# The last expert but one spread by a one-hot product, and the end of the kernel put in another order

## The chip, the cores and the metric

The kernel runs on one core of a Trainium2 chip. Its time is the device time of one execution in microseconds (us); the median of three runs stands for it. Engines are named as in the profile: PE is TensorE (matmuls), DVE is VectorE, ACT is ScalarE, POOL is GpSimd, SP is SyncE, which issues most DMAs. Each engine works through its own instructions in order; what waits at its head holds up all that stands behind.

## The reference

One layer of a latent backbone for 512 tokens of 1024 features: a gated linear attention mixer, then a mixture of 16 experts of which each token uses two, and a last RMSNorm. The change is in the experts and in the norm:

```python
for e in range(N_EXPERTS):
    he = jax.nn.silu(h @ w1[e]) * (h @ w3[e])
    out = out + gates[:, e:e + 1] * (he @ w2[e])
...
x = x + g2 * f.reshape(bsz, t, D_MODEL)
return _rmsnorm(x, final_g)
```

Each expert's w1, w3 and w2 are 2 MB each in float32, so all experts together read 96 MB.

## The kernel before

The experts are worked through one after another, the fullest ones first; which expert stands at which of the last 14 places is found at run time. In this text "expert 13" is the one at place 13 of the list `ex`, so experts 14 and 15 are the last two, with room for 32 tokens each; expert 13 has room for 64. Weights come in units of 1 MB, two for each of the parts a, b (gate and up weights, first and second half of the 1024 inputs) and d (down weights). `load_unit` issues a unit from SP; a manual dependency makes it wait until the unit three places back (two, from the 88th on) has landed. Units 88 and 89 are expert 14's d, 90 and 91 expert 15's a, 92 and 93 its b, 94 its first half of d; the other half comes as two half units.

Experts with more than 64 tokens (`Tile_`) have their weights split into a high and a low part on ACT and DVE (lines 56 and 57) and take three matmuls for one. Small experts (`Part`) use raw float32 weights (line 1202). Their tokens are gathered from `h2d` by POOL, turned on PE (1194), multiplied (1202), copied by ACT (`act`, 1210), turned again (1215), passed through SiLU on ACT and a product on DVE (`tr`, 1218 and 1219), multiplied with d, and scaled by the gate on DVE (`store`, 1227 or 1233). POOL then adds the rows into `accd` in DRAM by an indirect DMA (`scatter`, 1106). One scatter waits for the one before it.

At the end, `finish_load` reads the four tiles of 128 tokens back from `accd` (SP, line 1342), after the last scatter has landed; ACT sums their squares (`squares`, 1345); DVE scales them and SP writes them out. Expert 15 is not scattered: its rows of `accd` are gathered (`late_rows`), its own result is added (1381), these rows are normed by themselves and written over the output's rows by an indirect DMA (`late_store`, 1393). `finish_consts` sets aside freed weight buffers for all this and lays two constant rows out for expert 15 (`lay`, ACT copies of 32x256).

A list of small DVE steps, "bookkeeping" below, prepares a loop for tokens beyond the experts' room (lines 1457 to 1490); it stands behind `ex[10]`. With these inputs the loop runs zero times. Inside `manual_schedule(engines=tail)` the order of the code is the order on the engines; elsewhere a scheduler sets it.

Of the kernel before, what the change touches and what calls it, by code (L numbers as in the profile page):

```python
# [8 lines left out]
F32 = mybir.dt.float32  # L9
# [23 lines left out]
def dit_kernel(ctx: ExitStack, tc: tile.TileContext, I, out):  # L33
# [647 lines left out]
    def load_unit(u, e, s, hs=None):  # L681
        t = u[s] if s in u else free.pop(0)
        if t is None:
            t = stg.tile([P, 2048], F32, tag="st", name="st")
        w, v = (I[("w_gate_e", "w_up_e")[s % 2]], s // 2) if s < 4 else (I["w_down_e"], s - 4)
        w = w[0, e, v] if isinstance(e, int) else w[0, bass.ds(e, 1), v].rearrange("a p n -> (a p) n")
        h = slice(0, 2048) if hs is None else slice(1024 * hs.start, 1024 * hs.stop)
        d = nc.sync.dma_start(t[:, h], w[:, h])
        if len(dmas) >= 3 and not isinstance(e, int):
            back = 2 if hs is not None or len(dmas) >= 88 else 3  # L690
            tc.add_manual_dep(d.ins, dmas[-back].ins.name, mybir.DependencyInfo(mybir.DependencyClass.Sync, mybir.DependencyReason.DATA), reason="queue depth")
        dmas.append(d)
        u[s] = t
# [488 lines left out]

    class Part:
        def __init__(s, c, w):
            s.idx, s.gs, s.late, s.mark = gix2[:, c:c + 1], gsl[:, c:c + 1], None, None
# [26 lines left out]
        def tr(s):  # L1212
            pt = bank(pb)
            for k in range(s.nk):
                PE.transpose(pt[:, k * P:(k + 1) * P], s.he[:, k * P:(k + 1) * P], ident)
            pt = pt[:, 0:s.n].rearrange("p (k a t) -> p k a t", k=s.nk, a=s.A)
            s.hr = s.he[:, 0:s.n // 2].rearrange("p (k a t) -> p k a t", k=s.nk, a=s.A // 2)
            S.activation(s.hr, pt[:, :, 0:s.A // 2], AF.Silu)
            V.tensor_mul(s.hr, s.hr, pt[:, :, s.A // 2:s.A])
            s.py = bank()[:, 0:s.n]  # L1220

        def dn(s, kt, w):
# [90 lines left out]
    one = raw2[0:1, :]  # L1313
    ss3, rstd3 = R("ss3", [4]), R("rstd3", [4])
    fin = {}

    def finish_consts():
        f, e = free.pop(0), free.pop(0)
        fin["g"], fin["j"], fin["row"] = f[:, 0:1024], f[:, 1024:2048], f[0:1, 1024:2048]
        fin["y"], fin["z"] = [[u[:, h * 1024:h * 1024 + 1024] for u in (free.pop(0), free.pop(0)) for h in range(2)] for _ in range(2)]  # L1320
        fin["h"], fin["g2"], fin["y15"] = [e[:, k * 512:k * 512 + 512] for k in range(3)]
# [10 lines left out]
    def finish_g():  # L1332
        for a in range(2):
            sl = slice(a * 512, a * 512 + 512)
            pt = bank()
            PE.matmul(pt, one, fin["row"][:, sl], start=True, stop=True)
            S.copy(fin["g"][:, sl], pt)
        lay("h", fin["g"])
# [8 lines left out]
    def finish_rsqrt(t):  # L1347
        rsqrt(rstd3[:, t:t + 2], ss3[:, t:t + 2], 2, 1.0 / D, "a", between=(lambda: finish_mul(3)) if t else None)

    def finish_mul(t):  # L1350
        (V if t % 2 else G).tensor_mul(fin["z"][t], fin["y"][t], fin["g"])

    def finish(t):
        z, r = fin["z"][t], rstd3[:, t:t + 1]
        V.tensor_scalar(z, z, r, None, op0=OP.mult)
        nc.sync.dma_start(out[0, t * P:(t + 1) * P, :], z)

    def finish_half(t):
        squares(t)
        finish_mul(t)  # L1360
        if t == 0:
            finish_mul(1)
        squares(t + 1)
        finish_rsqrt(t)
        finish(t)
        finish(t + 1)

    QA = P // tiles[-1][2]
    SELP = wr.rearrange("p k e -> p (k e)")
# [3 lines left out]
        V.tensor_add(sv, sv, ia) if a else V.tensor_copy(sv, ia)  # L1373
    lrs = R("lrs", [1])

    def late_rows(t):
        t.z = xbuf()[:, 0:t.n]
        gather(t.z, parts(accd, t.A), t.idx, t.A * T)

    def late_add(t):  # L1380
        V.tensor_add(t.z, t.z, t.y)
# [39 lines left out]
    with tc.manual_schedule(engines=tail):  # L1421
        p_, q_ = ex[NE - 2:]
        p, q = p_.tls[0], q_.tls[0]
        p.late = mo.tile([P, D], F32, tag="t4", name="y", bufs=NY)[:, 0:p.n]
        q.late = fin["y15"][:, 0:q.n]
# [6 lines left out]
        for c in "uFab":  # L1432
            if c == "F":
                finish_load()
            elif c in "0123":
                finish_load([int(c)])
            else:
                load_unit(wts[NE - 1], regs[NE - 1], {"u": 4}.get(c, 5), {"a": range(1), "b": range(1, 2)}.get(c))
        late_rows(q)
# [12 lines left out]
    ctx2.enter_context(tc.issue_after(ex[10].mark.ins))  # L1452
    NB = 9
    cap = R("cap", [NE])
    tmp4 = rk16
# [20 lines left out]
    t64 = big2[:, 0:64]  # L1476
    for x in range(NB):
        V.scalar_tensor_tensor(t64, cr, float(x + 1), capb.rearrange("p b e -> p (b e)"), op0=OP.is_equal, op1=OP.mult)
        V.tensor_reduce(off[:, x:x + 1], t64, axis=AX.X, op=OP.add)
        V.tensor_scalar(t64, cr, float(x + 1), None, op0=OP.is_equal)  # L1480
        V.tensor_reduce(ohe[:, x], t64.rearrange("p (b e) -> p e b", b=4), axis=AX.X, op=OP.add)
        ob = ohe[:, x].unsqueeze(1).to_broadcast([P, 4, NE])
        V.tensor_mul(tmp4.rearrange("p (t e) f -> p t (e f)", t=4), zm, ob)
        V.tensor_reduce(pmo[:, x], tmp4.rearrange("p (t e) f -> p t (e f)", t=4), axis=AX.X, op=OP.add)
        V.tensor_mul(tmp4.rearrange("p (t e) f -> p t (e f)", t=4), oh[:, 1], ob)
        V.tensor_reduce(k1o[:, x], tmp4.rearrange("p (t e) f -> p t (e f)", t=4), axis=AX.X, op=OP.add)
# [53 lines left out]
```

## Time and profile before

| | us |
|---|---|
| median of three runs | 655.16 (655.14 to 655.5) |
| the profiled execution's own time | 656.5 |
| its span, first to last instruction | 654.7 |
| PE busy | 599.0 (91%) |
| DVE busy | 463.6 (71%) |
| ACT busy | 302.6 (46%) |

The profile shows one execution. A busy PE is one with matmuls in flight, which is not the same as PE at its peak; the granted clock stands in a column of its own. Busy shares are means over stages with different limits, so the end is read by itself below.

### The profile page before, as it was taken

To read this page: it belongs to the slowest core of one execution; us is meant where nothing else is said; L and a number is where in the kernel's file an instruction comes from. 1 tells how busy PE (TensorE), PEld (TensorE's weight loads), DVE (VectorE), ACT (ScalarE), POOL (GpSimd) and SP (SyncE) were. 2 spreads that over 40 slices of the span, in tenths; PEclk is the share of its full clock that TensorE was granted. 3 is DMA by queue.
4 is the path that set the end of the run, shared out by engine and by line. 5 is a ranking of instruction groups with operands and counts; after the bars stand their busy time and mean duration, and the time that the engine had idled before them with its cause. 6 is when DMAs were issued, how large, how long until landed. Compare 5 with 4: busy or idle time off the path is not lost. (4 is left out here: it accounts for less than half of the span.)

```text
span 654.7 us, 11203 instructions
## 1 busy us (share of the span) xinstructions
PE 599.0 (91%) x4200; PEld 412.4 (63%) x4200; DVE 463.6 (71%) x984; ACT 302.6 (46%) x511; POOL 98.3 (15%) x102
## 2 busy tenths in 40 slices
PE   3999999999999999999979989999999999999741
PEld 2778577776878878778748465545565657664310
DVE  5667499849985972575288399465767689999615
ACT  6433399257352233642451255334444457773131
POOL 4030000010100010012200330120322222222032
PEclk9999999999999999999998999999999999999975
DMA  8996472220234861658662989899999999999974
GB/s 269 340 353 218 175 274 66 67 66 4 67 130 158 270 232 51 254 183 354 237 227 74 373 316 366 326 342 351 412 387 395 362 352 358 393 383 345 298 273 189
DMA packets 50251, 168.41 MB, mean 257 GB/s; under 512 B 6779, under 2 KB 17237, under 8 KB 37138
## 3 DMA queue, kind: packets, MB, share of 16 engines
q1 hardware_dynamic: 43216, 156.26, 64.4%
q0 software_dynamic: 5024, 8.70, 5.6%
q10 hardware_dynamic: 1954, 2.71, 1.3%
q8 instruction: 34, 0.56, 0.3%
q14 instruction: 23, 0.19, 0.1%
HBM read 158.64 MB, written 12.30 MB: 261 GB/s over the span
## 5 line engine op out<-in xcount | busy, mean ns | idle before, releaser
L51 PE MATMUL bk<-wh,fh 128*128 128x512 f32 (+3 forms) x276 | 110.9, 409 | 0.7 <-ACT fh L56 0.4
L52 PE MATMUL bk<-wl,fh 128*128 128x512 f32 (+3 forms) x276 | 111.3, 405 | 0.0
L53 PE MATMUL bk<-wh,fl 128*128 128x512 f32 (+3 forms) x276 | 109.0, 399 | 0.5 <-DVE fl L57 0.5
L282 DVE TENSOR_TENSOR wl<-st,wh 128x512 fp32r<-128x512 f32 x60 | 39.9, 685 | 38.9 <-ACT wh L281 37.6
L56 ACT CAST wh<-su 128x1024 fp32r<-128x1024 f32 x45 | 46.8, 1047 | 39.9 <-PE bk L53 38.7
L281 ACT CAST wh<-st 128x512 fp32r<-128x512 f32 x60 | 35.9, 620 | 59.5 <-PE bk L53 50.8
L51 PEld LDWEIGHTS bk<-wh,fh 128*128 128x128 f32 (+3 forms) x276 | 50.2, 183 | 19.2 <-ACT wh L56 3.3
L57 DVE TENSOR_TENSOR wl<-su,wh 128x1024 fp32r<-128x1024 f32 x45 | 54.5, 1222 | 10.5 <-ACT wh L56 8.3
L1106 POOL DMA_INDIRECT accd<-y,gix x16 | 37.2, 2324 | 164.8 <-DVE y L1166 78.2
L52 PEld LDWEIGHTS bk<-wl,fh 128*128 128x128 f32 (+3 forms) x276 | 50.6, 183 | 16.5 <-issue 3.3
L53 PEld LDWEIGHTS bk<-wh,fl 128*128 128x128 f32 (+3 forms) x276 | 50.6, 183 | 13.7 <-issue 1.2
L1202 PE MATMUL bk<-su,he 128*64 128x512 f32 (+1 forms) x136 | 21.7, 526 | 12.5 <-DMA su<-in_w_down_e_dram 9.6
L1202 PE MATMUL bk<-su,xg 128*32 128x256 f32 (+1 forms) x216 | 31.7, 485 | 1.5 <-DVE xg L1196 1.5
L56 ACT CAST fx<-su 128x1024 fp32r<-128x1024 f32 x21 | 22.0, 1050 | 21.8 <-PE bk L53 21.6
L57 DVE TENSOR_TENSOR fx<-su,fx 128x1024 fp32r<-128x1024 f32 x21 | 25.7, 1222 | 7.4 <-ACT fx L56 7.2
L51 PE MATMUL bk<-fx,fh 128*128 128x512 f32 (+3 forms) x68 | 27.9, 410 | 1.2 <-ACT fh L56 1.2
L52 PE MATMUL bk<-fx,fh 128*128 128x512 f32 (+3 forms) x68 | 27.3, 402 | 1.0 <-DVE fx L57 1.0
L53 PE MATMUL bk<-fx,fl 128*128 128x512 f32 (+3 forms) x68 | 26.6, 394 | 0.2 <-DVE fl L57 0.2
L1102 POOL DMA_INDIRECT xg<-h2d,gix x16 | 20.1, 1259 | 39.2 <-DVE pis L1005 15.1
L250 POOL DMA_DIRECT2D mrd<-mrow x8 | 3.8, 487 | 129.2 <-DVE mrow L248 129.2
L1202 PEld LDWEIGHTS bk<-su,he 128*64 128x64 f32 (+1 forms) x136 | 6.6, 127 | 24.4 <-DMA su<-in_w_down_e_dram 11.0
L57 DVE TENSOR_TENSOR fl<-bk,fh 128x512 fp32r<-128x512 f32 (+3 forms) x25 | 15.5, 634 | 7.5 <-ACT fh L56 5.5
(476 smaller groups left out, 1303.6 us busy)
## 6 DMA issues: line engine op xcount, KB each, us to landing
su<-in_w_up_e_dram SPq DMA_DIRECT2D x23, 1024.0 KB, 8.2
su<-in_w_down_e_dram SPq DMA_DIRECT2D x21, 1024.0 KB, 7.8
su<-in_w_gate_e_dram SPq DMA_DIRECT2D x19, 1024.0 KB, 8.3
st<-in_gla_w_in_dram SPq DMA_DIRECT2D x10, 1024.0 KB, 5.0
QQ<-in_w_mod_dram SPq DMA_DIRECT2D x5, 1024.0 KB, 10.8
st<-in_w_gate_e_dram SPq DMA_DIRECT2D x5, 1024.0 KB, 6.8
st<-in_w_up_e_dram SPq DMA_DIRECT2D x5, 1024.0 KB, 9.0
B<-in_w_mod_dram SPq DMA_DIRECT2D x4, 1024.0 KB, 5.1
```

Of the source, the lines that this page charges most:

```text
L51: PE.matmul(o, ah, bh, start=first, stop=False)
L52: PE.matmul(o, ah, bl, start=False, stop=False)
L53: return PE.matmul(o, al, bh, start=False, stop=last)
L56: S.copy(hi, full)
L57: return V.tensor_sub(lo, full, hi.bitcast(F32))
L250: G.dma_start(mrd[4 * h_ + c4:4 * h_ + c4 + 1, :], mrow[32 * c4:32 * c4 + 1, :])
L281: S.copy(w[0][:, k], st[:, k])
L282: mark[0] = V.tensor_sub(w[1][:, k], st[:, k], w[0][:, k].bitcast(F32))
L1102: G.indirect_dma_start(out=xg, out_offset=None, in_=src, in_offset=bass.IndirectOffsetOnAxis(ap=idx, axis=0), bounds_check=n - 1, oob_is_e ...
L1106: G.indirect_dma_start(out=dst, out_offset=bass.IndirectOffsetOnAxis(ap=idx, axis=0), in_=y, in_offset=None, bounds_check=n - 1, oob_is_er ...
L1202: PE.matmul(o[s.w * a:s.w * a + s.w], l, r(a), start=first, stop=last, tile_position=(0, s.w * a))
```

## The change

- Queue depth: a unit's load waits for the unit three places back to the very end.
- Expert 14 is no longer scattered. Its result `p.late` is put as a high and a low half into two zeroed tiles of 128x1024 (`spread_pads`); a one-hot matrix of its token numbers spreads the rows over each of the four tiles of tokens by float32r matmuls (`spread_mm`, eight for the first two tiles between expert 15's parts a and b, eight behind them), and DVE adds them from PSUM to the tiles read back (`spread_add`). `finish_load` then waits for expert 13's scatter as the last one.
- Expert 15's rows are picked out of the four finished sums on PE by a second one-hot matrix (`late_rows`), not gathered from DRAM.
- The final norm's weights come by a DMA of 512 KB that repeats the row on all partitions (issued by ACT), in place of a row of 4 KB and matmuls with ones; they are laid out for expert 15 at the same place in `finish_consts`.
- Expert 15's SiLU is made from an exponential, an addition, a reciprocal and a product (`by_exp`); ACT's table is changed ahead of it. The final scaling is one DVE step for each tile instead of two; POOL no longer multiplies.
- The bookkeeping takes three blocks at a time and stands behind `ex[4]`.

```diff
-            back = 2 if hs is not None or len(dmas) >= 88 else 3
+            back = 3
...
+            if s.by_exp:
+                S.activation(s.hr, gate, AF.Exp, scale=-1.0)
+                V.tensor_scalar(s.hr, s.hr, 1.0, None, op0=OP.add)
+                V.reciprocal(s.hr, s.hr)
+                V.tensor_mul(s.hr, s.hr, gate)
...
     def finish_consts():
...
-        nc.scalar.dma_start(fin["row"], I["final_g"].rearrange("(o n) -> o n", o=1))
-        V.memset(one, 1.0)
+        nc.scalar.dma_start(fin["g"], I["final_g"].rearrange("(o n) -> o n", o=1).partition_broadcast(P))
         lay("g2", g2b)
+        lay("h", fin["g"])
...
+    def finish_out(t):
+        z = fin["y"][t]
+        V.scalar_tensor_tensor(z, z, rstd3[:, t:t + 1], fin["g"], op0=OP.mult, op1=OP.mult)
         nc.sync.dma_start(out[0, t * P:(t + 1) * P, :], z)
...
+    def spread_pads(t):
+        ph, pl = spread[0]
+        for a in range(t.A):
+            q, n = slice(t.w * a, t.w * a + t.w), slice(a * t.n, a * t.n + t.n)
+            S.copy(ph[q, n], t.y[q])
+            V.tensor_sub(pl[q, n], t.y[q], ph[q, n].bitcast(F32))
+
+    def spread_mm(k):
+        (ph, pl), hot = spread
+        bs = [bank(), bank()]
+        for a, b in enumerate(bs):
+            for p_, f in ((ph, True), (pl, False)):
+                PE.matmul(b, hot[:, k * P:k * P + P], p_[:, a * 512:a * 512 + 512], start=f, stop=not f)
+        return bs
+
+    def spread_add(k, bs):
+        for a, b in enumerate(bs):
+            y = fin["y"][k][:, a * 512:a * 512 + 512]
+            V.tensor_add(y, y, b)
...
-    def late_rows(t):
-        t.z = xbuf()[:, 0:t.n]
-        gather(t.z, parts(accd, t.A), t.idx, t.A * T)
+    def late_rows(t, k):
+        if k == 0:
+            t.rows = bank(pb)[:, 0:t.n]
+        t.groups(t.rows, fin["hot"][:, k], lambda a: fin["y"][k][:, a * t.n:a * t.n + t.n], k == 0, k == 3)
...
         p_.down(wts[NE - 2])
-        p_.scatter()
-        G.drain()
-        finish_g()
+        S.preload_act_table_set("natural_log_exp_and_others")
         q_.up(wts[NE - 1], "a")
+        spread_pads(p)
+        load_unit(wts[NE - 1], regs[NE - 1], 4)
+        finish_load()
+        for h in range(2):
+            load_unit(wts[NE - 1], regs[NE - 1], 5, range(h, h + 1))
+        bs = [spread_mm(k) for k in range(2)]
         q_.up(wts[NE - 1], "b")
...
         q_.turn()
-        S.preload_act_table_set("natural_log_exp_and_others")
-        for h in range(2):
-            finish_half(2 * h)
+        for k in range(2):
+            spread_add(k, bs[k])
+            squares(k)
+        bs += [spread_mm(k) for k in range(2, 4)]
+        for k in range(2):
+            late_rows(q, k)
+        finish_scale(0)
+        for k in range(2, 4):
+            spread_add(k, bs[k])
+            squares(k)
+            late_rows(q, k)
+        finish_out(0)
+        finish_out(1)
+        finish_scale(2)
         q_.down(wts[NE - 1])
         late_add(q)
         late_square(q)
+        finish_out(2)
+        finish_out(3)
         late_out(q)
         late_store(q)
...
-    ctx2.enter_context(tc.issue_after(ex[10].mark.ins))
+    ctx2.enter_context(tc.issue_after(ex[4].mark.ins))
```

**ACT around expert 13's turn.** Before, these rows stand on ACT one after another: `lay` of the gate row (1330), the DMA of the 4 KB row (1322), expert 13's `act` (1210) and its SiLU (1218). The names in brackets are the counters that a row waits for; DMAHW stands for a DMA of SP or ACT.

```order
L1330 COPY srg<-g1b 32x256 [waits DMAHW6_49,PE_49]
L1330 COPY srg<-g1b 32x256 x3
L1322 DMA srg<-in_final_g_dram 1x1024 [waits DMAHW5_49,DMAHW2_49,PE_49]
L1210 COPY he<-bk 128x512 [waits PE_49]
L1218 ACTIVATE he<-bk 128x256 [waits PE_49,Activation_49]
```

In the change the same place on ACT reads as follows (line 1330 is now the DMA of the final norm's weights, 1338 is `lay`, 1225 is expert 13's SiLU).

```order
L1330 DMA srg<-in_final_g_dram 128x1024 [waits DMAHW5_49,DMAHW1_49,PE_49]
L1338 COPY srg<-g1b 32x256 [waits DMAHW6_49,PE_49]
L1210 COPY he<-bk 128x512 [waits PE_49]
L1338 COPY srg<-g1b 32x256 x3
L1338 COPY srg<-srg 32x256 [waits DMAHW1_49]
L1338 COPY srg<-srg 32x256 x3
L1225 ACTIVATE he<-bk 128x256 [waits PE_49,Activation_49]
```

Four copies that read the landed weights (srg from srg, waiting for a DMA) now stand ahead of expert 13's SiLU.

**DVE from expert 15's turn on.** In the change DVE's rows at the end are these (1221 to 1226 are expert 15's SiLU and product, 1392 the additions of the spread rows, 136 to 129 the steps of the reciprocal root).

```order
L1221 TENSOR_SCALAR he<-he 128x128 [waits Activation_49]
L1222 RECIPROCAL he<-he 128x128 [waits DVE_49]
L1223 TENSOR_TENSOR he<-he,bk 128x128 [waits DVE_49,PE_49]
L1226 TENSOR_TENSOR he<-he,bk 128x128 [waits DVE_49]
L1392 TENSOR_TENSOR B_86<-B_86,bk 128x512 [waits DMAHW7_49,DMAHW5_49]
L1392 TENSOR_TENSOR B_86<-B_86,bk 128x512
L1392 TENSOR_TENSOR B_86<-B_86,bk 128x512 [waits DMAHW6_49]
L1392 TENSOR_TENSOR B_86<-B_86,bk 128x512
L136 TENSOR_SCALAR rsv<-ss_3376 128x2 [waits Activation_49]
L127 TENSOR_TENSOR rst<-rstd_3377 128x2 [waits Activation_49]
```

Before, expert 15's one product (1219) stood there, and right behind it the first product of the final scaling; all additions of the spread rows now stand behind expert 15's turn.

## Rows read from the trace of the kernel before

**Rows 1.** Stages by engine: window, length, busy times, PE's clock, DMA share, GB/s.

```profile
572.00:588.00 16.00, 15.70 (x72) 9.98 (x71) 15.71 (x23) 12.61 (x14) 3.50 (x3) 1.00 1.00 385
601.40:608.00 6.60, 6.06 (x53) 2.37 (x53) 6.46 (x41) 2.19 (x5) 1.46 (x1) 1.00 0.94 296
624.00:630.00 6.00, 4.24 (x46) 1.69 (x38) 0.00 (x0) 0.37 (x1) 1.56 (x1) 0.85 0.68 222
636.00:642.00 6.00, 1.08 (x8) 0.20 (x8) 5.58 (x7) 4.34 (x10) 4.11 (x2) 0.50 0.83 301
```

**Rows 2.** The end in time order: start, length, instruction, idle time before it and releaser.

```profile
630.26 2.03 SPq L1342 DMA_DIRECT2D B<-accd  x2
634.11 1.06 ACT L1345 ACTIVATE srg<-B 128x1024 f32<-128x1024 f32 x1 [2.43 <-issue]
642.51 1.08 PE L1202 MATMUL bk<-su,he 128*32 128x256 f32 x8 [0.74 <-DMA su<-in_w_down_e_dram]
645.74 0.48 DVE L1227 SCALAR_TENSOR_TENSOR srg<-bk,gsl,srg 128x256 f32<-128x256 f32 x1
647.89 0.16 DVE L136 TENSOR_SCALAR rsv<-bk 128x1 f32<-128x1 f32 x1 [1.22 <-PE bk L1388]
649.20 0.48 DVE L1390 SCALAR_TENSOR_TENSOR xg<-xg,lrs,srg 128x256 f32<-128x256 f32 x1
649.98 1.06 POOL L1393 DMA_INDIRECT out_dram<-xg,gix  x1 [9.35 <-DVE xg L1390]
```

**Rows 3.** The scatters of experts 13 and 14: start, and time from issue to landing.

```profile
L1106 POOL DMA_INDIRECT accd<-y,gix x1: 1563/1563/1563, 615.4 to 615.4; - x1
DMA to landing us min/median/max: 9.9/9.9/9.9
...
L1106 POOL DMA_INDIRECT accd<-y,gix x1: 1558/1558/1558, 626.0 to 626.0; - x1
DMA to landing us min/median/max: 4.2/4.2/4.2
```

**Rows 4.** Experts 13 to 15 on ACT and PE in time order, columns as in rows 2.

```profile
603.37 1.64 ACT L1330 COPY srg<-g1b 32x256 f32<-32x256 f32 x4 [5.00 <-PE bk L1202]
608.57 0.38 ACT L1218 ACTIVATE he<-bk 128x256 f32<-128x256 f32 x1 [2.61 <-PE bk L1215]
609.90 3.65 PE L1202 MATMUL bk<-su,he 128*64 128x512 f32 x16 [1.42 <-DVE he L1219]
613.48 1.93 PE L1202 MATMUL bk<-su,xg 128*32 128x256 f32 x32
617.12 1.93 PE L1202 MATMUL bk<-su,he 128*32 128x256 f32 x32 [0.75 <-DVE he L1219]
621.85 3.23 PE L1202 MATMUL bk<-su,xg 128*32 128x256 f32 x32 [0.52 <-DVE xg L1196]
```

**Rows 5.** Other transfers' time to landing: two of 512 KB from ACT, one gather of 128 KB.

```profile
L1096 ACTq DMA_DIRECT2D g1b<-mrd x1: 326/326/326, 339.3 to 339.3; - x1
DMA to landing us min/median/max: 3.7/3.7/3.7
...
L648 ACTq DMA_DIRECT2D g1b<-mrd x1: 597/597/597, 284.6 to 284.6; - x1
DMA to landing us min/median/max: 5.7/5.7/5.7
...
L1102 POOL DMA_INDIRECT xg<-h2d,gix x1: 1487/1487/1487, 591.3 to 591.3; - x1
DMA to landing us min/median/max: 10.1/10.1/10.1
```

**Rows 6.** Nearest DVE steps to those that are new, in time order or with min, median, max.

```profile
345.84 0.55 DVE L906 RECIPROCAL sc<-sc 128x64 f32<-128x64 f32 x1
357.42 1.28 DVE L842 SCALAR_TENSOR_TENSOR h<-h,rstd,xg 128x1024 f32<-128x1024 f32 x1
...
L717 DVE TENSOR_TENSOR srg<-bk,g1b x8: 681/684/691, 306.3 to 338.6; 128x512 f32<-128x512 f32 x8
```

More of the change, by code (lines that the diff above doesn't have):

```diff
@@ L1184, in __init__ @@
         def __init__(s, c, w):
-            s.idx, s.gs, s.late, s.mark = gix2[:, c:c + 1], gsl[:, c:c + 1], None, None
+            s.idx, s.gs, s.late, s.mark, s.by_exp = gix2[:, c:c + 1], gsl[:, c:c + 1], None, None, False
             s.w, s.A = w, P // w
@@ L1217, in tr @@
             s.hr = s.he[:, 0:s.n // 2].rearrange("p (k a t) -> p k a t", k=s.nk, a=s.A // 2)
-            S.activation(s.hr, pt[:, :, 0:s.A // 2], AF.Silu)
-            V.tensor_mul(s.hr, s.hr, pt[:, :, s.A // 2:s.A])
+            gate, up = pt[:, :, 0:s.A // 2], pt[:, :, s.A // 2:s.A]
+            if s.by_exp:
[3 more added lines that the diff above has]
+                V.tensor_mul(s.hr, s.hr, gate)
+            else:
+                S.activation(s.hr, gate, AF.Silu)
+            V.tensor_mul(s.hr, s.hr, up)
             s.py = bank()[:, 0:s.n]
@@ L1318, in finish_consts @@
         f, e = free.pop(0), free.pop(0)
-        fin["g"], fin["j"], fin["row"] = f[:, 0:1024], f[:, 1024:2048], f[0:1, 1024:2048]
-        fin["y"], fin["z"] = [[u[:, h * 1024:h * 1024 + 1024] for u in (free.pop(0), free.pop(0)) for h in range(2)] for _ in range(2)]
-        fin["h"], fin["g2"], fin["y15"] = [e[:, k * 512:k * 512 + 512] for k in range(3)]
-        nc.scalar.dma_start(fin["row"], I["final_g"].rearrange("(o n) -> o n", o=1))
-        V.memset(one, 1.0)
+        fin["g"], fin["j"] = f[:, 0:1024], f[:, 1024:2048]
+        fin["y"] = [u[:, h * 1024:h * 1024 + 1024] for u in (free.pop(0), free.pop(0)) for h in range(2)]
+        fin["h"], fin["g2"] = [e[:, k * 512:k * 512 + 512] for k in range(2)]
+        fin["late"] = [e[:, 1024 + 256 * k:1280 + 256 * k] for k in range(3)]
+        fin["hot"], fin["xi"] = e[:, 1792:1920].rearrange("p (t s) -> p t s", t=4), e[:, 1920:1922]
+        nc.scalar.dma_start(fin["g"], I["final_g"].rearrange("(o n) -> o n", o=1).partition_broadcast(P))
         lay("g2", g2b)
+        lay("h", fin["g"])
     def lay(name, src):
@@ L1330, in lay @@
             S.copy(fin[name][q, 0:n], src[q, a * n:a * n + n])
[L1332 to L1338, printed above, removed]
     def finish_load(ts=range(4)):
@@ L1359, in finish_half, with spread_consts @@
         squares(t)
-        finish_mul(t)
-        if t == 0:
-            finish_mul(1)
         squares(t + 1)
-        finish_rsqrt(t)
-        finish(t)
-        finish(t + 1)
+        finish_scale(t)
+        finish_out(t)
+        finish_out(t + 1)
+    def spread_consts(t):
+        pads = [x[:, 0:1024] for x in (fh, fl)]
+        hot, xi, c = fh[:, 1024:1536], fin["xi"], cols[order[NE - 2]][0][0]
+        for x in pads:
+            G.memset(x.bitcast(F32), 0.0)
+        for k, o in enumerate((1.0, -255.0)):
+            V.tensor_scalar(xi[:, k:k + 1], ixf[:, c:c + 1], o, None, op0=OP.add)
+            V.tensor_scalar(hot[:, 256 * k:256 * k + 256], iot, xi[:, k:k + 1], None, op0=OP.is_equal)
+        for k in range(4):
+            V.tensor_scalar(fin["hot"][:, k], iot[:, 0:32], zp[:, k, ND - 1:ND], None, op0=OP.is_equal)
+        return pads, hot
+    def spread_pads(t):
[15 more added lines that the diff above has]
+            V.tensor_add(y, y, b)
     QA = P // tiles[-1][2]
@@ L1374, in dit_kernel @@
     lrs = R("lrs", [1])
-    def late_rows(t):
-        t.z = xbuf()[:, 0:t.n]
-        gather(t.z, parts(accd, t.A), t.idx, t.A * T)
+    def late_rows(t, k):
+        if k == 0:
+            t.rows = bank(pb)[:, 0:t.n]
+        t.groups(t.rows, fin["hot"][:, k], lambda a: fin["y"][k][:, a * t.n:a * t.n + t.n], k == 0, k == 3)
     def late_add(t):
-        V.tensor_add(t.z, t.z, t.y)
+        t.z = fin["late"][2]
+        V.tensor_add(t.z, t.y, t.rows)
     def late_square(t):
@@ L1423, in dit_kernel @@
         p, q = p_.tls[0], q_.tls[0]
-        p.late = mo.tile([P, D], F32, tag="t4", name="y", bufs=NY)[:, 0:p.n]
-        q.late = fin["y15"][:, 0:q.n]
+        p.late, q.late = fin["late"][0:2]
+        q.by_exp = True
+        spread = spread_consts(p)
+        G.drain()
         p_.down(wts[NE - 2])
-        p_.scatter()
-        G.drain()
-        finish_g()
+        S.preload_act_table_set("natural_log_exp_and_others")
         q_.up(wts[NE - 1], "a")
-        q_.up(wts[NE - 1], "b")
[L1432 to L1439, printed above, removed]
-        q_.turn()
-        S.preload_act_table_set("natural_log_exp_and_others")
-        for h in range(2):
-            finish_half(2 * h)
+        spread_pads(p)
[4 more added lines that the diff above has]
+        bs = [spread_mm(k) for k in range(2)]
+        q_.up(wts[NE - 1], "b")
+        q_.turn()
+        for k in range(2):
[12 more added lines that the diff above has]
+        finish_scale(2)
         q_.down(wts[NE - 1])
@@ L1475, in dit_kernel @@
     pmo, k1o = [f.rearrange("p (x t) -> p x t", x=NB) for f in (sc.rearrange("p t e -> p (t e)")[:, 0:4 * NB], big2[:, 512 - 4 * NB:512])]
[L1476 to L1486, printed above, removed]
+    NX3 = 3
+    for x in range(0, NB, NX3):
+        xs = slice(x, x + NX3)
+        bx = big2[:, 0:64 * NX3].rearrange("p (x n) -> p x n", x=NX3)
+        bt = big2[:, 0:64 * NX3].rearrange("p (x t e) -> p x t e", x=NX3, t=4)
+        wide = lambda a, n: a.unsqueeze(1).to_broadcast([P, NX3] + n)
+        V.scalar_tensor_tensor(bx, wide(cr, [64]), -1.0, iof[:, xs].unsqueeze(2).to_broadcast([P, NX3, 64]), op0=OP.add, op1=OP.is_equal)
+        V.tensor_reduce(ohe[:, xs], bx.rearrange("p x (b e) -> p x e b", b=4), axis=AX.X, op=OP.add)
+        V.tensor_mul(bx, bx, wide(capb.rearrange("p b e -> p (b e)"), [64]))
+        V.tensor_reduce(off[:, xs], bx, axis=AX.X, op=OP.add)
+        for dst, src in ((pmo, zm), (k1o, oh[:, 1])):
+            V.tensor_mul(bt, wide(src, [4, NE]), ohe[:, xs].unsqueeze(2).to_broadcast([P, NX3, 4, NE]))
+            V.tensor_reduce(dst[:, xs], bt, axis=AX.X, op=OP.add)
     V.tensor_mul(big2[:, 0:NB * NE].rearrange("p (x e) -> p x e", x=NB), ohe, iof.unsqueeze(1).to_broadcast([P, NB, NE]))
@@ L1498, in dit_kernel @@
         index_of(0, [(0, 0, P)], lambda e_: pmx, lambda e_: rv[:, :, 0])
+        p.scatter()
         q.scatter()
-        V.tensor_scalar(gix2[:, NTL - 1:NTL], gix2[:, NTL - 1:NTL], 2 * q.A * T, None, op0=OP.add)
+        V.tensor_scalar(gix2[:, NTL - 2:NTL], gix2[:, NTL - 2:NTL], 2 * q.A * T, None, op0=OP.add)
         o, u = Expert([(0, P)]), {}
```

10 lines of the change are left out of this document (2 added, 8 removed).

## The prediction

> **What bounds the kernel now.** I read the table of stages first. Until about 594 us everything is full: in the 16 us from 572 PE is busy 15.70, DVE 15.71, and the DMA engines' share is 1.00 at 385 GB/s. From 601 the rate falls to 296 GB/s, from 624 PE works 4.24 of 6 us, and from 636 almost not at all [rows 1]. So the time that this change can move lies behind 600 us, and there the rows in time order say what ends last.
>
> Two chains meet there. [...] The other is the data's: expert 13's scatter is issued at 615.4 and lands 9.9 us later, at 625.3; only then may expert 14's go (626.0, landing 4.2 later, 630.2) [rows 3]; at 630.26 SP starts to read the sums back, at 634.11 ACT has the first tile, and the last weights, which stand behind these reads on SP, let PE go on at 642.51. DVE is still busy with the final scaling and takes expert 15's result at 645.74; its late rows leave at 649.98, and the span ends at 654.7, 4.72 us later [rows 2].
>
> **What the change takes away.** (1) The reads wait for expert 13's scatter alone: at the old places 625.3 instead of 630.2, so 4.9 us come free on the data's chain. (2) With depth 3 to the end the weights from unit 88 on are issued one landing earlier, and the rate can stay nearer 385 than 296 GB/s. In PE's chain that is worth nothing before expert 15's b, since PE up to there waits for ACT and DVE [rows 4]. (3) The bookkeeping leaves 588 to 613 us, where DVE is busy 6.46 of 6.60 us [rows 1]. It held up expert 13's product, so that PE came 1.33 us after the SiLU's start (608.57 to 609.90); without it 0.95 (0.38 for ACT, some 0.4 for DVE, gaps). Around experts 5 to 8, where it goes, PE is the one waited for; I take nothing there, with 0 to 1 us as bounds.
>
> **What it puts in their place: first a wait on ACT.** The four copies of the final norm's weights stand ahead of expert 13's SiLU, and they wait for 512 KB from DRAM. That DMA can be issued once the first half of expert 13's up b is through: the copies of before were let go by the same matmuls at 603.37 [rows 4], and the DMA needs one matmul less (0.46 us, two records of 3.65/16), so 603.0. Landing is the unknown. ACT's own transfers of that size took 3.7 and 5.7 us, but with one unit of weights or none queued; in the full stretch a gather of only 128 KB took 10.1 us [rows 5], and expert 13's scatter 9.9 [rows 3]. In the change three units are under way at 603, so I take 7.5 us, nearer the full stretch, with 3.7 and 10.1 as bounds. Then: landing 610.5, four copies of 1.64 us in all [rows 4] to 612.2, SiLU, and PE's down matmuls at 613.1 instead of 609.90. That is **+3.2 us** on PE's chain; behind expert 13's SiLU wait, in order, expert 13's store and scatter, both matmul stages of expert 14, and with them all of expert 15.
>
> [...]
>
> **The clock.** PE would then stand idle from about 608.5, where the turn of expert 13 ends, to 613.1. [...] Bounds 0 and 3.6; I take **+1.0**, since it came back within some 3 us the last time. Expert 13 is then through at 613.1 + 3.65 + 1.0 = 617.8.
>
> **Then PE's chain to expert 15's turn.** Expert 14's up b 1.93, turn and SiLU 1.71 (615.41 to 617.12), down 1.93 [rows 4]: 623.4. Expert 15's rows are turned and copied; before, that and the matmuls with ones took 2.80 us (619.05 to 621.85). Without the ones about 1.0: 624.4, and here 0.9 us are won. Up a 1.93 (not 3.23, at full clock): 626.3. The eight spread matmuls of 512 columns, 0.23 us each by the 16 records of 3.65 us: 628.2. Their pads are ready by then (ACT and DVE copy during up a). Up b 1.93: 630.1. The weights of b are issued two landings earlier than before and are there. The turn took 1.6 us before (629.1 to the matmuls at 630.7). The exponential's way adds a reciprocal over 128 columns, 2 x 0.55 = 1.1 [rows 6], an addition and a product, together 1.75: turn over at 633.45.
>
> **Then DVE's chain.** The spread additions stand behind that turn. Each tile takes two steps of 0.68 from PSUM [rows 6], 1.38 together. Two tiles: 2.75. The square on ACT (1.06 and 0.19 for its sum) and the root (logarithm, exponential and three small steps, 1.31 from 647.89 to 649.20) hold DVE up, about 2.55 together: 5.3. Two more tiles: 8.05. Two final scalings of 1.28 [rows 6] at a pitch of 1.25, and the second root's DVE steps 0.85: 11.4. [...] I take 12.0 for the meeting of both: expert 15's result on DVE at 645.4, against 645.74. All that the data's chain won has by then been spent.
>
> Is the data late? Expert 13's scatter goes 1.84 us after its down matmuls (613.55 to 615.4), so at 619.6; with 8 us to landing the reads start at 627.6, the first tile is there 3.85 us later (630.26 to 634.11), 631.5, and the last weights 12.25 later, 639.9. Both are earlier than DVE and PE want them. Only with more than 9.5 us does it begin to cost.
>
> **And the end.** Expert 15's rows (0.48 + 0.42), then the last two scalings, 2.5, now stand ahead of the last root on DVE. The last tile is issued 3.75 us after 645.4 and lands 3 us later (an estimate from the writes of before); the late rows overwrite the same output and wait for it: 6.9 us after DVE took the result, not 4.24 (645.74 to 649.98) [rows 2]. With the same 4.72 to the end: 645.4 + 6.9 + 4.72 = **657.0**.
>
> **The sum.** 657.0 against the span of 654.7 is +2.3 us. The profiled execution took 656.5 with 1.8 us outside its span, which the change doesn't touch; the runs' median is 655.16. So I predict 655.16 + 2.3 = **657.5 us**. Differences under 0.2% (1.3 us) of this kernel can't be told from none.
>
> **Rivals.**
> *The 512 KB land at once, no change.* With 5.7 us and no loss of clock the sum is shorter by 1.8 + 1.0: 654.2 for the span, 654.7 for the median. For it: ACT's transfer at 284.6, and its queue of its own. Against: DMA share 0.94 here [rows 1] and three units ahead. Chance 0.25, with all that ends within 0.2%.
> *Faster: the weights land before ACT wants them.* ACT has the gate row's copies to make until about 607.2 anyway. If the DMA lands within 4.2 us, the wait is gone: SiLU at 608.85, PE at 609.8, the clock holds, and everything runs 3.3 + 1.0 earlier: 652.7 for the span, 653.2 for the median. Row 339.3 with 3.7 us is for it [rows 5], though nothing else was moving then. This is the point that decides: every us of landing beyond 4.2 puts one us on the end, and the gain is gone at about 5. Chance 0.2.
> *The scatter is late.* If expert 13's scatter lands 14 us after issue, the reads start at 633.6, the last weights come at 645.9, and the span ends near 660. It is the upper part of my own case, as are a landing of 10.1 (+2.6) and a low clock in expert 15's a, spread and b (up to +5). All together would be beyond 661; I leave that out.
>
> **How the numbers follow.** Slower, by a landing of 5.7 to 10.1 us: chance 0.55, its own range 656.5 to 661. Same 0.25, faster 0.20. The range to hold eight in ten has to reach into the faster case: 653.0 to 661.0, which leaves most of that case's lower half and the sum of all mishaps outside.
>
> **What would show it.** On ACT a wait of 2 to 4 us for a DMA ahead of the copies at line 1338, and expert 13's SiLU after 611. On PE an idle stretch from about 608.5 to 613. The reads from `accd` at 626 to 629, before 630.26 (step 1 right). No waits of PE for the weights of expert 15's b. DVE in one run of work from expert 15's turn to its result, some 11 to 12 us. The late rows' DMA waiting for the last output tile. The prediction is wrong if the 512 KB land by 608, if DVE's additions don't stand behind the turn, or if PE's clock stays at one level throughout the end.

## The result, and the profile after

The change makes the kernel slower: 664.74 us (664.21 to 666.81, four runs) against 655.33 us beside it, a ratio of 1.013 with a 95% interval of 1.0098 to 1.0162. The profiled execution took 664.97 us with a span of 663.2, against 656.5 and 654.7 before. The direction was forecast (657.5 us, slower by 2.3); the size was not, and the time lies outside the range of 653 to 661.

ACT around expert 13's SiLU, in time order, in the changed kernel (start, length, engine and line; in brackets the idle time ahead and what ended it):

```profile
604.32 0.35 ACTq L1330 DMA_DIRECT2D srg<-in_final_g_dram  x1
604.76 0.40 ACT L1338 COPY srg<-g1b 32x256 f32<-32x256 f32 x1 [5.42 <-PE bk L1202]
606.05 0.58 ACT L1210 COPY he<-bk 128x512 f32<-128x512 f32 x1 [0.89 <-PE bk L1202]
606.66 1.23 ACT L1338 COPY srg<-g1b 32x256 f32<-32x256 f32 x3
614.27 1.64 ACT L1338 COPY srg<-srg 32x256 f32<-32x256 f32 x4 [6.38 <-DMA srg<-in_final_g_dram]
615.93 0.38 ACT L1225 ACTIVATE he<-bk 128x256 f32<-128x256 f32 x1
```

ACT stands still for 6.38 us until the final norm's weights have landed, 9.9 us behind their issue, and expert 13's SiLU comes at 615.93; it was at 608.57 before [rows 4]. That is the wait that was forecast, longer. PE's rows of the same stretch and on to expert 15's second part:

```profile
602.35 3.65 PE L1202 MATMUL bk<-srg,xg 128*64 128x512 f32 x16
...
616.83 5.73 PE L1202 MATMUL bk<-su,he 128*64 128x512 f32 x16 [6.78 <-DVE he L1226]
622.49 1.93 PE L1202 MATMUL bk<-su,xg 128*32 128x256 f32 x32
...
632.90 1.93 PE L1202 MATMUL bk<-st,xg 128*32 128x256 f32 x32
```

The down matmuls of expert 13 start at 616.83, not 609.90, and take 5.73 us for what took 3.65. The stages (window, length, busy time of PE, PE's weight loads, DVE, ACT and POOL, PE's granted clock, DMA share, GB/s) say why:

```profile
602.30:609.00 6.70, 6.38 (x50) 2.46 (x51) 2.76 (x11) 2.19 (x5) 1.47 (x1) 1.00 0.98 375
609.00:616.80 7.80, 1.05 (x13) 0.35 (x5) 0.42 (x1) 1.99 (x5) 0.00 (x0) 0.84 0.68 209
616.80:624.00 7.20, 7.17 (x44) 2.46 (x48) 1.37 (x2) 0.00 (x0) 0.00 (x0) 0.70 1.01 422
```

In the 7.8 us of the wait PE works 1.05 us; after it the granted clock is 0.70 on the mean: read by the us, it is 0.50 from 615 to 621 us and 1.00 again from 622. The DMA rate falls too, to 209 GB/s. The list of SP's waits in 600 to 640 us (line, what it waited for, total, times, longest) has the reason, which the forecast had not seen:

```profile
SPq L688 <- DMA srg<-in_final_g_dram: 9.6, 1, 9.6
```

The program shows the link. The load that waits is this one, in SP's order of the change:

```order
L688 DMA su_2693<-in_w_up_e_dram 128x2048 [waits DMAHW6_49,DMAHW1_49,PE_49]
```

It waits for DMAHW1, the counter on which ACT's transfer lands (the copies of `lay` wait for the same name): from its load at 604.23 to the next at 614.35 us SP issues nothing.

The end, from expert 15's last product on (DVE, then the late rows on POOL):

```profile
637.82 0.29 DVE L1226 TENSOR_TENSOR he<-he,bk 128x128 f32<-128x128 f32 x1
638.02 2.47 DVE L1392 TENSOR_TENSOR B<-B,bk 128x512 f32<-128x512 f32 x4
...
642.82 2.48 DVE L1392 TENSOR_TENSOR su<-su,bk 128x512 f32<-128x512 f32 x4
645.22 2.47 DVE L1352 SCALAR_TENSOR_TENSOR B<-B,rstd,srg 128x1024 f32<-128x1024 f32 x2
...
649.23 0.48 DVE L1234 SCALAR_TENSOR_TENSOR srg<-bk,gsl,srg 128x256 f32<-128x256 f32 x1 [1.00 <-PE bk L1202]
...
650.08 2.47 DVE L1352 SCALAR_TENSOR_TENSOR su<-su,rstd,srg 128x1024 f32<-128x1024 f32 x2
...
653.77 0.48 DVE L1418 SCALAR_TENSOR_TENSOR srg<-srg,lrs 128x256 f32<-128x256 f32 x1
```

The late rows on POOL:

```profile
658.08 1.05 POOL L1421 DMA_INDIRECT out_dram<-srg,gix  x1 [32.10 <-SPq L1535]
```

DVE has expert 15's result at 649.23 and its late rows ready at 654.25, yet they go at 658.08. POOL's queue waits twice ahead of them, until 654.8 and until 657.3:

```profile
L1421 POOLq EVENT_SEMAPHORE  x2: 43/43/43, 654.8 to 657.3; - x2
```

The two waits end with the landings of the last two output tiles, issued at 651.39 and 652.58. The last one is late in one part only: of the sixteen steps in which the trace counts this tile's landing, fifteen come by 655.28, 2.7 us behind the issue, and the last at 657.23. This is what the DMA engines moved from 654 to 657.3 us (busy tenths in 40 slices, then each queue's packets, MB and share):

```profile
DMA  9999898981000300002000101101010100000000
q1 hardware_dynamic: 97, 0.33, 25.5%
q8 instruction: 1, 0.02, 1.8%
```

From 655 us on the DMA engines stand nearly idle, at 16 GB/s until 657 and at 0 from there to 658. Among the tile's packets stands one of 16 KB on the queue that the profile calls instruction, from 654.20 to 655.15; the tile's last eight packets follow it one after another, from 655.14 to 656.77, while nothing else moves. In e1, e5 and e6 below the late rows go 5.49 to 5.58 us behind the issue of the last tile, here 5.50; in e7 the last two tiles land 2.7 us behind their issue. That the 16 KB are the cause is an assumption of mine: no run moves them alone.

To compare kernels I cut the span at two places: the start of expert 13's up b on PE, and expert 15's last product on DVE (line 1219 or 1226).

| kernel | start of up b | up b to last product | last product to the end |
|---|---|---|---|
| before | 601.39 | 29.0 | 24.3 |
| the change | 602.35 | 35.5 | 25.4 |

So of the 8.5 us in the span some 6.5 lie in the middle, around the wait, 1.1 in the end and 1.0 ahead of both.

### The profile page after: what moved, and what is told of

Read it like the earlier page. It is cut to its first block, busy times and chain, and to the rows that moved or that the text cites. A ratio compares the mean times of both kernels' runs of the same rounds, so it can differ in the third digit from the quotient of the medians.

```text
span 663.2 us, 11260 instructions
## 1 busy us (share of the span) xinstructions
PE 607.3 (92%) x4244; PEld 417.9 (63%) x4244; DVE 467.7 (71%) x956; ACT 303.0 (46%) x513; POOL 91.5 (14%) x100
## 5 line engine op out<-in xcount | busy, mean ns | idle before, releaser
L57 DVE TENSOR_TENSOR wl<-su,wh 128x1024 fp32r<-128x1024 f32 x45 | 54.5, 1221 | 8.2 <-ACT wh L56 6.9
L1202 PE MATMUL bk<-su,he 128*64 128x512 f32 (+1 forms) x136 | 25.1, 572 | 7.5 <-DVE he L1226 7.5
L57 DVE TENSOR_TENSOR fx<-su,fx 128x1024 fp32r<-128x1024 f32 x21 | 25.6, 1221 | 5.6 <-ACT fx L56 5.3
L1202 PEld LDWEIGHTS bk<-su,he 128*64 128x64 f32 (+1 forms) x136 | 9.1, 145 | 20.1 <-issue 10.7
L1240 DVE SCALAR_TENSOR_TENSOR y<-bk,gsl,g1b 64x512 f32<-64x512 f32 (+1 forms) x14 | 9.4, 672 | 16.7 <-PE bk L1202 16.6
```

The lines of the kernel that those rows point to most:

```text
L57: return V.tensor_sub(lo, full, hi.bitcast(F32))
L1202: PE.matmul(o[s.w * a:s.w * a + s.w], l, r(a), start=first, stop=last, tile_position=(0, s.w * a))
L1240: s.mark = V.scalar_tensor_tensor(y[q], s.py[q], s.gs[q], g2b[q, a * s.n:a * s.n + s.n], op0=OP.mult, op1=OP.mult)
```

## The experiments

**Theory A**: ACT's wait for the 512 KB ahead of expert 13's SiLU, with the clock that it costs, carries nearly all of the loss. **Rival B**: the weights that SP could only issue from 614.35 on would have held PE anyway. **Rival C**: the loss is in the end, in DVE's order and the late rows' wait. Each kernel is compared with the kernel before on the same chip; as the chips differ (it took 656.52, 657.04 and 657.08 us on the three of the experiments), experiments are set against each other by their ratios to it.

### e1: the four copies behind expert 14's spread

```diff
     def finish_consts():
...
         lay("g2", g2b)
-        lay("h", fin["g"])
...
         spread_pads(p)
+        lay("h", fin["g"])
```

> Edit: the four copies that lay out final_g for expert 15 stand on ACT behind the spread of expert 14 (behind its four copies into the padded tile), not ahead of expert 13's SiLU; the 512 KB transfer itself is issued where it was, and SP's next load still waits for it. Theory A (ACT's wait for the 512 KB transfer ahead of expert 13's SiLU carries the loss): SiLU of expert 13 near 605 us in place of 615.9, its down product at full clock (3.6 to 3.9 us), and the time falls by 6 to 8 us, to 656.5 to 658.5 us. Rival B (the weights of expert 15, which SP could issue only from 614.35 us on because it waited for the same transfer, hold TensorE anyway): TensorE waits for them ahead of the two up products of expert 15, and the time falls by less than 4 us, to over 660.5 us. Rival C (the loss lies in the tail, on VectorE and in the last store): under 2 us, over 662.5 us.

Measured: 658.03 us, ratio 1.0029 (1.0008 to 1.005). The transfer still took 9.1 us and SP still waited for it (its loads go at 604.24 and 614.00), but ACT did not:

```profile
610.64 0.38 ACT L1225 ACTIVATE he<-bk 128x256 f32<-128x256 f32 x1 [2.25 <-PE bk L1215]
```

PE in the same kernel, expert 13's down and expert 15's up a:

```profile
611.53 3.65 PE L1202 MATMUL bk<-su,he 128*64 128x512 f32 x16 [0.99 <-DVE he L1226]
...
621.63 1.93 PE L1202 MATMUL bk<-su,xg 128*32 128x256 f32 x32 [0.57 <-DVE xg L1196]
```

The clock holds (1.00 from 602 to 620 us), expert 13's down matmuls take 3.65 us, and PE never waits for a weight. The middle part is 27.6 us instead of 35.5, the end 25.6. A stands: 1.0 of the 1.3% that the change lost, some 6.6 us by the ratios, are its; B falls. My 605 us for the SiLU was wrong: the turn on PE (line 1215) is ready only at 610.6, since the scheduler had put expert 14's up a between its transposes.

### e2: the wait alone, put into the kernel before

```diff
-        nc.scalar.dma_start(fin["row"], I["final_g"].rearrange("(o n) -> o n", o=1))
-        V.memset(one, 1.0)
+        nc.scalar.dma_start(fin["g"], I["final_g"].rearrange("(o n) -> o n", o=1).partition_broadcast(P))
         lay("g2", g2b)
+        lay("h", fin["g"])
...
-        finish_g()
```

> Edit in the kernel before: final_g comes as one 512 KB transfer on ACT's queue, spread over the partitions, and its four copies stand on ACT ahead of expert 13's SiLU, as in the change; the two products with ones and their copies go; all else is as before (scatter, gather, queue depth 2, bookkeeping behind the eleventh expert). Theory A: this wait alone is enough: the landing takes 8 to 11 us, the down product of expert 13 starts 7 to 9 us later, and the time rises by 6 to 9 us to 661 to 664.5 us. Rival C (the tail, the depth or the bookkeeping is what costs): 654.5 to 657 us.

Measured: 662.43 us, ratio 1.0092 (1.0064 to 1.0119), +6.0 us against the 656.52 beside it: the low end of what A gave. The landing took 9.3 us; ACT and PE read like those of the change:

```profile
612.23 1.64 ACT L1330 COPY srg<-srg 32x256 f32<-32x256 f32 x4 [5.76 <-DMA srg<-in_final_g_dram]
```

And PE:

```profile
614.79 5.13 PE L1202 MATMUL bk<-su,he 128*64 128x512 f32 x16 [6.16 <-DVE he L1219]
```

The wait is enough for most of the loss, without the spread, the new end or the bookkeeping, and SP issues a load at 606.96, while the transfer is under way (602.89 to 612.2), and the next only at 612.97, 0.8 us behind its landing, so it is ACT's wait. Two things came out otherwise than expected. Expert 13's down matmuls start 4.9 us later than before, not 7 to 9. And the delay does not stay in the middle: in the profile, whose execution of 659.94 us is the quickest of the four, the middle is 30.7 us (29.0 before) and the end 26.4 (24.3), where the reads from `accd` start at 632.76 instead of 630.26, behind a later scatter of expert 14. So the path from the wait to the end is another one than in the change.

### e3: the bookkeeping behind the eleventh expert again

```diff
-    ctx2.enter_context(tc.issue_after(ex[4].mark.ins))
+    ctx2.enter_context(tc.issue_after(ex[10].mark.ins))
```

> Edit: the bookkeeping stands behind the eleventh expert again, as before; all else as in the change. If the bookkeeping's place makes the 0.9 us by which TensorE is late from 493 us on: the up product of expert 13 starts near 601.4 us in place of 602.35, and the time falls by about 0.9 us, to 663.5 to 664.2 us. If the 0.9 us have another cause: 602.3 us, and 664.7 us as for the change. If the wider bookkeeping now gets in the way of the late experts: over 666 us.

Measured: 663.65 us, ratio 1.0104 (1.007 to 1.0139), up b of expert 13 at 601.94. That leans to the first answer, but the interval overlaps the change's. See e11.

### e4: queue depth 2 as before

```diff
-            back = 3
+            back = 2 if hs is not None or len(dmas) >= 88 else 3
```

> Edit: the queue depth falls to 2 from the 88th weight unit on, as before; all else as in the change. If the 512 KB transfer lands late because it shares the DMA engines with the units that are queued ahead of it (three at depth 3, two at depth 2): it lands 2 to 4 us sooner, 6 to 8 us behind its issue in place of 9.9, and the time falls by 1.5 to 4 us, to 661 to 663 us. If its landing doesn't hang on the depth: 9 to 11 us, and 664 to 666 us.

Measured: 662.27 us, ratio 1.0077 (1.0046 to 1.0108). The landing took 6.3 us, and ACT waited 2.77 us instead of 6.38:

```profile
611.51 1.64 ACT L1338 COPY srg<-srg 32x256 f32<-32x256 f32 x4 [2.77 <-DMA srg<-in_final_g_dram]
```

PE behind it:

```profile
614.07 5.15 PE L1202 MATMUL bk<-su,he 128*64 128x512 f32 x16 [3.17 <-DVE he L1226]
```

As expected if the units under way set the landing. But e2, also at depth 2, had 9.3 us, so the depth alone does not. And behind PE's wait of 3.17 us the granted clock is 0.50 from 614 to 616 us and 0.72 to 618: the matmuls take 5.15 us, nearly as long as the 5.73 behind a wait of 6.78.

### e5: the transfer on POOL's queue

```diff
-        nc.scalar.dma_start(fin["g"], I["final_g"].rearrange("(o n) -> o n", o=1).partition_broadcast(P))
+        G.dma_start(fin["g"], I["final_g"].rearrange("(o n) -> o n", o=1).partition_broadcast(P))
```

> Edit: the 512 KB transfer of final_g is issued by POOL, on its own queue and its own counters, not by ACT; the four copies stay ahead of expert 13's SiLU. POOL issues it behind expert 12's scatter, near 607 us. So ACT still waits, and SP's next load no longer has to wait for this transfer. Theory A (ACT's wait is what costs; SP's is covered by it): SiLU of expert 13 as late as in the change or later (615 to 618 us), ratio to before 1.010 to 1.017. Rival B (SP's wait, and with it the late weights, is a loss of its own): the time falls by 2 us or more against the change, ratio under 1.010.

Measured: 663.63 us, ratio 1.0091 (1.0058 to 1.0123). The edit did something else than I had written: the scheduler put the four copies one place further on, behind expert 13's SiLU (609.97) and ahead of expert 14's `act`. The landing took 13.0 us there:

```profile
620.82 1.64 ACT L1338 COPY srg<-srg 32x256 f32<-32x256 f32 x4 [10.47 <-DMA srg<-in_final_g_dram]
622.49 0.37 ACT L1210 COPY he<-bk 128x256 f32<-128x256 f32 x1
```

The ratio is in the range that I had given to B, but as the wait was moved it doesn't test B. It shows that a wait of ACT one expert later, here 10.47 us and with SP issuing freely, costs about as much: the intervals of the two kernels overlap.

### e6: e1 and e5 together, neither ACT nor SP waits

> Edit: e1's (the four copies behind the spread of expert 14) and the transfer on POOL's queue: neither ACT nor SP waits for it. If the three weight units that SP issues at once when it is let go (614.0, 614.6, 615.2 us in e1) are what makes expert 13's scatter land 9.8 us after its issue, that scatter lands in 5 to 8 us here, the reads start near 624 us in place of 626.9, and the time is 1 to 2 us under e1's: ratio to before 0.999 to 1.002. If not: 9 to 10 us, and e1's ratio of 1.003.

Measured: 656.97 us, ratio 1.0006 (0.9981 to 1.0031), which overlaps e1's. Expert 13's scatter still landed 9.1 us behind its issue: the three units that SP issues at once in e1 are not what makes it late. With both waits gone the rest of the change is worth nothing measurable. Nor does SP's freedom bring the weights sooner to where PE wants them: PE waits for expert 15's part b here and not in e1, and the middle is 28.7 us against 27.6.

```profile
626.14 1.92 PE L1202 MATMUL bk<-st,xg 128*32 128x256 f32 x28 [1.67 <-DMA st<-in_w_up_e_dram]
```

### e7: e1, and the last two tiles written ahead of expert 15's result

```diff
         finish_scale(2)
+        finish_out(2)
+        finish_out(3)
         q_.down(wts[NE - 1])
         late_add(q)
         late_square(q)
-        finish_out(2)
-        finish_out(3)
```

> Edit: e1's, and the final scaling and writing of the last two tiles stand on DVE and SP ahead of expert 15's result, not behind it. Theory C (what is left of the loss is that the late rows wait for the last output tile, 3.8 us after DVE has them ready in e1): the last tile is written 1.5 to 2 us sooner, DVE's last row comes 1.5 to 2 us later and the two meet: the time falls by 1.5 to 2.5 us against e1, ratio to before 0.999 to 1.001. If the wait for the last tile is not what ends last: no change or up to 2 us slower, ratio 1.003 to 1.006.

Measured: 656.23 us, ratio 0.9992 (0.9973 to 1.0011), about 2.4 us under e1 by the ratios, whose intervals just touch. In e1 the last rows stand on DVE at 646.81 and the late rows leave 4.31 us later:

```profile
646.81 0.48 DVE L1417 SCALAR_TENSOR_TENSOR srg<-srg,lrs 128x256 f32<-128x256 f32 x1
```

POOL in e1:

```profile
651.12 1.05 POOL L1420 DMA_INDIRECT out_dram<-srg,gix  x1 [32.52 <-SPq L1535]
```

In e7 it is 0.77 us, and POOL waits for DVE, no longer for a landing:

```profile
648.77 0.48 DVE L1417 SCALAR_TENSOR_TENSOR srg<-srg,lrs 128x256 f32<-128x256 f32 x1
```

POOL in e7:

```profile
649.54 1.05 POOL L1420 DMA_INDIRECT out_dram<-srg,gix  x1 [29.62 <-DVE srg L1417]
```

The end takes 22.8 us instead of e1's 25.6. C is real, but it is the smaller part. Two things changed at once, though: the tile goes ahead of expert 15's result, and its landing takes 2.7 us, where e1's rows leave about 4.6 (the late rows go 5.49 us behind the issue; 0.85 of that, as in the change, lies between the landing and POOL's start). By an estimate from e1's rows (issue 645.63, 2.7 to the landing, 0.85 more to POOL) its late rows would have gone at 649.2 with e7's landing, 1.9 us sooner. So most of the gain may be this, and e7 doesn't part the two.

### e8: e6 and e7 together, the bookkeeping behind the eleventh expert

> Edit: e1's, e6's and e7's together, and the bookkeeping behind the eleventh expert. The sum of the parts: e1 less 1 to 2 us by the free queue, less 1.5 to 2.5 by the order of the end, less 0 to 0.9 by the bookkeeping: 2.5 to 5 us under e1, ratio to before 0.995 to 0.999, faster than before. If the parts cover each other (reads and DVE both end last): ratio 0.999 to 1.002.

Measured: 653.56 us, ratio 0.9948 (0.9929 to 0.9968): faster than the kernel before and the change. Up b at 602.57, the middle 26.4 us, the end 22.2.

### e9: e8 with expert 15's SiLU in one step

```diff
-        q.by_exp = True
...
-        S.preload_act_table_set("natural_log_exp_and_others")
         q_.up(wts[NE - 1], "a")
...
         q_.turn()
+        S.preload_act_table_set("natural_log_exp_and_others")
```

> Edit: the combined kernel (e8) with expert 15's SiLU on ACT in one step, as for the other experts, and the change of ACT's table behind it. If DVE's additions wait for expert 15's turn alone, the 1.5 us that the exponential's way takes longer (addition 0.23, reciprocal 0.95, product 0.29) come off the end: ratio to before 0.992 to 0.9935, against 0.995 for e8. If the tiles read back land no sooner than the additions start in e8 (629.2 us, 3.5 us behind the first read), the additions only wait for them instead: 0 to 0.6 us, ratio 0.994 to 0.9955. If the table's change (1.28 us) now delays the squares: slower than e8, over 0.9955.

Measured: 653.93 us, ratio 0.9954 (0.9918 to 0.9991), no gain that can be told. In its profile the gain is hidden ahead of the turn, by the last weights of part b, and behind it, by the tile read back:

```profile
625.37 1.92 PE L1202 MATMUL bk<-st,xg 128*32 128x256 f32 x28 [1.69 <-DMA st<-in_w_up_e_dram]
```

DVE in e9:

```profile
630.73 1.28 DVE L1391 TENSOR_TENSOR B<-B,bk 128x512 f32<-128x512 f32 x2 [0.41 <-DMA B<-accd]
```

### e10: e8 with the last tile scaled by POOL and ACT

```diff
+        fin["z"] = free.pop(0)[:, 0:1024]
...
+        G.tensor_mul(fin["z"], fin["y"][3], fin["g"])
         finish_out(0)
...
-        finish_out(3)
+        S.activation(fin["z"], fin["z"], AF.Copy, scale=rstd3[:, 3:4])
+        nc.sync.dma_start(out[0, 3 * P:4 * P, :], fin["z"])
```

> Edit: the combined kernel (e8) with the last tile's scaling taken from DVE: POOL multiplies it with the final weights into a buffer of its own while ACT takes the squares, ACT multiplies it with the root. One DVE step of 1.24 us ahead of expert 15's result goes. If DVE's order at the end is what ends last: 0.9 to 1.3 us off, ratio to before 0.993 to 0.994. If POOL's product slows DVE's steps beside it (in the trace of before a DVE product of 1.22 us took 2.18 beside POOL's) or the last tile then comes later by way of POOL and ACT: no gain or up to 1.5 us slower than e8, ratio 0.995 to 0.9975.

Measured: 655.57 us, ratio 0.9979 (0.9947 to 1.0011): no gain, and 0.3% more than e8, just beyond the second answer, though the two intervals overlap. POOL's product and DVE's two scalings beside it, in e10:

```profile
637.42 3.33 POOL L1479 TENSOR_TENSOR su<-su,srg 128x1024 f32<-128x1024 f32 x1 [20.40 <-DVE su L1392]
```

DVE in e10:

```profile
637.25 4.58 DVE L1352 SCALAR_TENSOR_TENSOR B<-B,rstd,srg 128x1024 f32<-128x1024 f32 x2
```

They take 4.58 us where they took 2.48 alone in e8: of the two scalings the second ends only at 641.83, behind POOL's product, which ends at 640.75. A DVE step of 1.24 is saved and 2.1 are lost. PE also waits 1.10 us for part b's weights here, which it does not in e8, so the ratio is not the price of this alone.

### e11: e8 with the bookkeeping behind the fifth expert

> Edit: the combined kernel (e8) with the bookkeeping behind the fifth expert, as in the change. If its place costs about 1 us ahead of expert 13 (in the profiles so far the up product of expert 13 starts at 602.3 to 604.2 us in six kernels with it there, at 600.9 to 602.6 in four with it behind the eleventh): that product at 602.9 to 604.2 us, ratio to before 0.996 to 0.9975. If those profiles only scatter: about 602 to 602.6 us and e8's ratio, 0.9945 to 0.9955.

Measured: 654.48 us, ratio 0.9961 (0.9928 to 0.9994); its profile fell on its longest run (659.58), with up b already at 608.15, so it doesn't tell the cases apart. All profiles together: up b at 600.9 to 602.6 in six kernels with the bookkeeping behind the eleventh expert, at 602.3 to 604.2 in six with it behind the fifth, and 608.15 here. That speaks for some 1 us; e3 and e11 by their times (0.26% and 0.13%, each inside the intervals) don't contradict it and don't prove it.

## Why the prediction was right in direction and wrong in size

**What bounds the kernel, and the two chains.** Right: PE's own chain, expert by expert, and the data's. The reads of `accd` no longer wait for expert 14 and start at 629.18, a little ahead of 630.26 although expert 13 was 7 us late; the data's chain ended nothing.

**The wait on ACT.** Right as a mechanism, shown by e1 (taken away) and e2 (put in alone). Its size was the mis-sized term: a landing of 7.5 us against 9.9. The issue was also 1.3 us later than 603.0, of which 0.96 is the later start of up b. So the copies came at 614.27, not 610.5. The upper bound, 10.1 us from the gather [rows 5], was the better row: 9.9, 9.1 and 9.3 us in the change, e1 and e2, 9.8 and 9.0 in e3 and e7, 6.3 only in e4. A landing of 5.7 us like that of ACT's transfer at 284.6 [rows 5], the first rival, came in none of the runs, whose shortest is 6.3; nor does any of them show that a queue of its own, which that rival names, brings a transfer in sooner.

**The clock.** The second mis-sized term: 5.73 us for 3.65 is +2.1, where +1.0 was taken, with 0 and 3.6 as bounds, the upper one for a clock of 0.50 throughout, as it was from 636 to 642 before [rows 1]. No run shows the +1.0, an estimate of mine: in its place e2 and e4 showed +1.5, e3 +2.5. e4 shows that a wait half as long costs nearly as much clock (5.15), and e1 that behind a wait of 0.99 us nothing is lost (granted clock 1.00, 3.65 us). The length of the wait alone does not set the price: e2 waited 6.16 us and paid 5.13, e3 6.60 and 6.13.

**Bookkeeping at no cost.** Probably short by the whole upper bound, 0.96 us in the profile; not settled (e3, e11).

**PE's chain to expert 15's turn.** Right to 0.1 us: from 622.49 to the end of the turn at 638.1 it took 15.6 us, where 617.8 to 633.45 was forecast, 15.65, at a granted clock of 1.00 from 622 to 638 and with no wait for weights. That SP was held by the same counter was missed altogether, and cost nothing that e1 could show: PE did not wait for those weights. Where SP was free, in e6, PE did wait for them, 1.67 us; so "the weights of b are there" held in the change only because PE came late.

**DVE's chain.** From the turn to expert 15's result 11.1 us, where the forecast's times (633.45 to 645.4) give 11.95: 0.8 too much. The 12.0 taken there lies between DVE's own 11.4 and a time of PE that no run shows; in its place the change showed PE at a granted clock of 0.50 from 639 to 648, and a wait of DVE for it of 1.00 us ahead of expert 15's result.

**The end.** The wait for the last output tile was forecast; its size was the third mis-sized term: 8.85 us from DVE's result to the late rows, not 6.9. The last tile was issued 3.4 us behind the result (3.75 was forecast), but its landing was seen only at 657.3, some 4.7 us later rather than 3, with the 16 KB shown above among its packets. e7 takes this wait away.

**The sum.** +0.96 for the start, +0.36 for the issue, +2.4 landing, +1.0 clock (the next matmuls start 5.66 us behind, where 4.65 was taken), −0.8 DVE, +2.0 last store and +0.4 behind it make 6.3; between the forecast span of 657.0 and the measured one of 663.2 lie 6.2, the rest is rounding. Another 1 us lies in the frame: the profiled execution of before was 1.3 us over its median, that of the change 0.2.

**The range.** The terms that failed are the landing (7.5 against 9.9 us), the clock (+1.0 against +2.1) and the last store (6.9 against 8.85), and then the way in which they were bounded. Landing and clock were inside their bounds, 3.7 to 10.1 us and 0 to 3.6; the last store and the issue had none. My own case's upper end of 661 is the landing's bound (657.5 + 2.6 = 660.1) with under 1 us left for all else. What I named as beyond 661 and left out was another set, a late scatter, a landing of 10.1 and a low clock in expert 15's a, spread and b; of it only the landing came. Two of the terms are not independent: the clock's loss follows from the wait that the landing makes (e1 has neither). Bounds that rise together have to be added, not thinned out. The last store rose apart from these, when little else was under way (16 GB/s from 655 to 657 us), and nothing in the forecast bears on it.

**The rivals.** "At once, no change" and "faster" needed 5.7 and 4.2 us and got 9.9. "The scatter is late" didn't come: 4.7 us. When it went, at 624.40, SP had issued its last load at 620.55 and issued none until 629.18; no run shows whether that is the reason.

## What to carry to other kernels

Work that waits for a transfer should stand on its engine at the place where its result is used, not where the transfer is issued: four copies of 1.64 us, whose result is used at 653.77, cost 6.6 us, and moving one line gave them back. Where a small store overwrites part of a large one, the large one belongs ahead of the last computation (2.4 us here, of which the shorter landing of the last tile may be 1.9). And a fair price for a transfer beside a full queue was here the slowest row of its size or smaller, with what follows from it added: 10.1 us against 9.0 to 9.9 on ACT's queue, though not enough for POOL's, with 11.9 to 13.0.

## What the runs showed that I had not expected

- SP waited 9.6 us for a transfer of ACT's because both counted on DMAHW1; DMA traffic fell to 209 GB/s in the middle of the weights.
- A broadcast of 512 KB took 11.9 to 13.0 us on POOL's queue (e5, e6, e8: 13.0, 12.4, 11.9), 9.0 to 9.9 on ACT's (6.3 in e4). These runs differ in more than the queue: in e5, e6 and e8 SP issued four more units of 1 MB while it was under way, in the change and e1 none.
- TensorE's granted clock was 0.50 behind a wait of 3.17 us (e4) as it was behind one of 6.78: 5.15 and 5.73 us for the same sixteen matmuls, 3.65 without a long wait.
- In the change the last store's landing took 4.65 us, with a packet of 16 KB of another queue among its own, where the first two tiles' took 2.7. What the cause is no run shows.
- What sets the landing is not settled. The change and e1 (depth 3) had 9.9 and 9.1 us, e4 (depth 2) 6.3, but e2 (depth 2) 9.3.
